# Latent projections in a new order, grouped keys copied out first, and both key parts in one 512-column score product, in a four-layer decoder on one core

## The chip, the cores and the metric

One core of one Trainium2 chip runs the whole program. The metric is the time of one execution in microseconds (us) on the device. The kernel before took 2579.66 us, the median of three runs (2578.66 to 2579.76).

## What is computed

The reference is a decoder trunk of four layers on a sequence of 256 positions with 2048 features, all in float32. The layers mix the positions in three ways, in the order latent, sparse, window, latent. Each layer has one input projection, its own heads, four heads of attention over a memory of 256 rows, a gate, and one output projection:

```python
def reference(x, mem, ...):
    mem_n = _rmsnorm(mem, mem_norm)
    for i in range(DEPTH):
        h = _rmsnorm(x, norm_in[i])
        kind, j = i % N_MIXERS, i // N_MIXERS
        if kind == 0:
            self_out, mq, gate = _mla_branch(h, w_in_a[j], a_q_norm[j], w_uq[j], a_kv_norm[j], w_ukv[j])
        elif kind == 1:
            self_out, mq, gate = _dsa_branch(h, w_in_b[j], rel_bias)
        else:
            self_out, mq, gate = _swa_branch(h, w_in_c[j], c_sinks[j], rel_bias)
        mem_out = _memory_attention(mq, mem_n @ w_mem_kv[i])
        y = jnp.concatenate([self_out, mem_out], axis=-1) * jax.nn.silu(gate)
        x = x + y @ w_out[i]
    return _rmsnorm(x, final_norm)
```

In a latent layer 16 heads get their queries from a compressed query stream (1536 features, weights w_uq) and their keys and values from a compressed stream (512 features, weights w_ukv):

```python
    q = (_rmsnorm(c_q, q_norm) @ w_uq).reshape(B, S, A_HEADS, A_NOPE + A_ROPE)
    kv = (_rmsnorm(c_kv, kv_norm) @ w_ukv).reshape(B, S, A_HEADS, A_NOPE + A_V)
    ...
        s = (jnp.einsum('bqhd,bkhd->bhqk', qn, k_nope, preferred_element_type=jnp.float32)
             + jnp.einsum('bqhd,bkd->bhqk', qr, k_rope, preferred_element_type=jnp.float32)) * scale
```

The sparse and the window layer have 32 query heads in four groups that share keys and values, and add a relative-position bias to the scores. The sparse layer also has a small indexer, whose products choose 64 keys for each query. Softmax, the product with the values, the gate and the output projection are alike in all.

## The kernel before

**Numbers in pairs.** TensorE multiplies numbers of reduced precision (fp32r), so a float32 number is kept as two, a high and a low part: `split` (L67) makes the high part by a copy on ACT (L60) and the low part by a subtraction on DVE (L69). A product of two matrices is then three: high by high, high by low, low by high.

**The stream of weights.** All weights flow through the core once. `stage` (L210) loads a block over SyncE's queue into one of five buffers; the queue follows the order of the program. `parts_of` splits 512 columns of it into wh and wl, with three buffers each. TensorE reads them at once: `rows_by` (L244) makes six products of 512 columns of such a part (L261, L262, L263), `columns_by` (L266) makes four of 512 (L282, wh by both parts of the input) and four of 256 (L286, wl by the high part). The result goes to an accumulator in PSUM with the tag "acc", of which there are **two**. Whoever asks for a third waits until the first is read out. Small results, scores among them, go to four other buffers, tag "mp".

**Reading an accumulator.** `head_parts` (L319) makes a pair from an accumulator of `columns_by`, which keeps high and low sums apart: a copy on ACT, a subtraction on DVE (L323, tile zl) and an addition on DVE (L324).

**A latent part.** Each of the two latent layers runs four parts of four heads. `Latent.project` makes the queries in two halves (12 blocks of features, tile qn), the keys in two halves (4 blocks, kn), the values (`rows_by`, va and vf), in every second part the rotary queries (acc_qr), and the gate (acc_g). `Latent.attend` then makes scores, softmax and outputs.

**A grouped layer.** `Grouped.first` makes keys and values (acc_kv). `dup` writes the keys twice beside each other, as high and low parts (hl), from the accumulator, for transposing (tile tr, then kd); the values are copied to vs, from the same accumulator, behind the keys of their block. The indexer of the sparse layer follows (acc_iq, L306, L309).

**Scores and softmax.** The 256 positions are two blocks b of 128. For b = 0 only 128 keys count: one product takes the high and the low part of 128 keys, 256 columns side by side, and DVE adds the halves (L542). For b = 1 the high and the low part of 256 keys are 256 columns each, and TensorE sums them itself, as separate products into the same 256 columns (L762 latent, L956 grouped, L602 memory). DVE then makes the sum with bias or mask and its extreme in one pass (L544, or L603 in the memory heads), ACT the exponential (L549, L554, L607).

**What sets the order.** The program runs the parts 4, 0, 1, 2, 3, 5 (4 and 5 are the memory heads) and puts the output projection of the part before (`w_out`, acc_wo, added to xc by DVE at L1149) behind the attention of the next. Inside, a scheduler orders each engine's instructions by their expected times; the loads on SyncE's queue stay as written.

Of the kernel before, what the change touches and what calls it, by code (L numbers as in the profile page):

```python
# [8 lines left out]
F32 = mybir.dt.float32  # L9
# [22 lines left out]
def kernel(ctx: ExitStack, tc: tile.TileContext, a: dict, out: bass.AP,  # L32
# [20 lines left out]
    def f32(ap):  # L53
        return ap.bitcast(F32)
# [272 lines left out]
    class Norm:  # L327
# [37 lines left out]
        def finish(self):  # L365
# [5 lines left out]
            nc.vector.tensor_scalar(self.eighth, self.rstd, 0.125, None, op0=OP.mult)  # L371
            half = small("xh", 2)
# [157 lines left out]
    def masked_softmax(score, bias, scale=None, nsk=None):  # L530
# [5 lines left out]
        for b in range(2):  # L536
# [4 lines left out]
            if b == 0:  # L541
                nc.vector.tensor_add(u[:, :n], sp[:, n:2 * n], bi)  # L542
                bi = u[:, :n]
            nc.vector.tensor_tensor_reduce(u[:, :n], sp[:, :n], bi, -1.0,  # L544
# [46 lines left out]
    def memory_attend(nm, kT, v, qT, gT):  # L591
        y = act.tile([P, 2, 4, S], F32R, name="y", tag="y", bufs=2)
        for h in range(2):
            es = []
            mn, sm = small("mn", 2), small("sm", 2)
            for b in range(2):
                sp = misc("msp")
                qs = slice(b * P, (b + 1) * P)
                seq = [(qT[h][:, u, k, qs], kT[h][:, v_, k, :])
                       for k in range(2) for u, v_ in ((0, 0), (0, 1), (1, 0))]  # L600
                for n_, (l, r_) in enumerate(seq):
                    nc.tensor.matmul(sp[:, :S], l, r_, start=n_ == 0, stop=n_ == len(seq) - 1)  # L602
                nc.vector.tensor_reduce(mn[:, b:b + 1], sp[:, :S], AX.X, OP.max, negate=True)  # L603
# [3 lines left out]
                nc.scalar.activation(e, sp[:, :S], AF.Exp, bias=ms[:, :1], scale=nm.col("rstd", b),  # L607
# [34 lines left out]
    class Latent:  # L642
# [79 lines left out]
        def project(self, g):  # L722
# [7 lines left out]
            for half in range(2):  # L730
                acc = columns_by(self.cT[:3], 12, wq, 0, (g * 768 + half * 384, 2, 192, 0, A_NOPE), "qn")
                q = act.tile([P, 2, 2, S], F32R, name="qn", tag="pq", bufs=PQ)
                head_parts(q, acc)
                qn.append(q)
            for half in range(2):
                acc = columns_by(self.cT[3:], 4, wkv, 0, (g * 1024 + half * 512, 2, 256, 0, A_NOPE), "kn")
                k = act.tile([P, 2, 2, S], F32R, name="kn", tag="pq", bufs=PQ)
                head_parts(k, acc)
                kn.append(k)
            acc = rows_by(self.cT[3:], 4, wkv, 0, (g * 1024, 4, 256, A_NOPE, A_NOPE), "va")  # L740
            split(v[:, 0, :], v[:, 1, :], acc[:, 0, :])
            copy_act(vf, acc[:, 1, :])
            if g % 2 == 0:
                self.rotary(g)
            return qn, self.qr[g % 2], kn, (v[:, 0], v[:, 1], vf), gate(self.nm, self.w, self.g0 + g * 512)

        def attend(self, qn, qr, kn, v, gT):
            y = act.tile([P, 2, 4, S], F32R, name="y", tag="y", bufs=2)
            for h in range(4):
                def score(b):  # L750
# [6 lines left out]
                    else:  # L757
                        seq = [(q[:, 0, z, qs], k[:, 0, z, :]), (q[:, 0, z, qs], k[:, 1, z, :]),
                               (q[:, 1, z, qs], k[:, 0, z, :]),
                               (qr[:, h, qs], self.kr[:, 0, :]), (qr[:, h, qs], self.kr[:, 1, :])]  # L760
# [475 lines left out]
```

## Time and profile before

| | |
|---|---|
| median of three runs | 2579.66 us |
| the profiled execution | 2579.56 us |
| its span in the trace | 2577.8 us |
| TensorE (PE) | busy 2560.7 us, 14176 products |
| VectorE (DVE) | busy 1900.4 us, 3780 instructions |
| ScalarE (ACT) | busy 1596.3 us, 3240 instructions |
| GpSimd (POOL) | busy 81.9 us |

The span lies 1.8 us below the profiled execution's own time; that stretch is in no trace. PE is TensorE's products, PEld its loads of the stationary operand, which run beside the products. SP is SyncE. L282 is line 282 of the kernel; a name such as acc_kn<-cT,wh is the tile written and the tiles read.

### The profile page before, as it was taken

Reading aid. Unit: us, or ns where it says so; the run is one execution under the profiler, and the core shown is the slowest. Engines: PE = TensorE matmul, PEld = TensorE weight load, DVE = VectorE, ACT = ScalarE, POOL = GpSimd, SP = SyncE. Lnnn points to the kernel's source line nnn. Section 1 sums busy time; section 2 is a strip of 40 time slices with the busy share of each in tenths; the row PEclk is TensorE's granted clock in tenths of the full one; section 3 lists DMA queues with packets and bytes.
Section 4 is the critical chain, followed back from the end, with each engine's and each line's share of the span. In section 5 each row is a group of like instructions: output and inputs, shape, how many; then the busy total and the mean of one; then the engine's idle time right before and its main releaser. Section 6 shows DMA issues by size and latency. Waiting matters only on the chain.

```text
span 2577.8 us, 41377 instructions
## 1 busy us (share of the span) xinstructions
PE 2560.7 (99%) x14176; PEld 2213.9 (86%) x14176; DVE 1900.4 (74%) x3780; ACT 1596.3 (62%) x3240; POOL 81.9 (3%) x151
## 2 busy tenths in 40 slices
PE   9999999999999999999999999999999999999998
PEld 7888888888888889888888888888888888888887
DVE  6666667677777687988887777878867767777666
ACT  6556556556565566666676566666756656666555
POOL 1000000000000000000000000000000000000000
PEclk9999999999999999999999999999999999999999
DMA  9888778666667777566666575565655768676755
GB/s 300 250 264 259 245 213 236 172 180 189 196 187 220 204 219 228 170 197 184 208 188 188 172 220 172 173 188 165 199 161 163 233 186 208 195 193 172 218 168 186
DMA packets 477747, 519.99 MB, mean 202 GB/s; under 512 B 69424, under 2 KB 389824, under 8 KB 475872
## 3 DMA queue, kind: packets, MB, share of 16 engines
q1 hardware_dynamic: 460080, 449.71, 59.5%
q0 software_dynamic: 16736, 66.65, 8.0%
q8 instruction: 111, 1.82, 0.3%
q10 hardware_dynamic: 720, 0.98, 0.1%
q14 instruction: 100, 0.82, 0.1%
HBM read 494.10 MB, written 35.75 MB: 206 GB/s over the span
## 4 chain that ended last, share of the span: by engine, by line
PE 96%; DVE 2%; ACT 1%; DMA 0%; issue 0%; SPq 0%; ACTq 0%; DVEq 0%
PE acc_g L282 14%; PE acc_g L286 7%; PE acc_wo L262 7%; PE acc_wo L261 7%; PE acc_wo L263 7%; PE acc_mq L282 5%; PE acc_q L282 5%; PE acc_mk L282 5%; PE acc_cq L282 3%; PE acc_qn L282 3%; PE acc_mq L286 2%; PE acc_q L286 2%; PE acc_mk L286 2%; PE acc_mv L262 2%; PE acc_mv L261 2%; PE acc_mv L263 2%
## 5 line engine op out<-in xcount | busy, mean ns | idle before, releaser
L60 ACT ACTIVATE wh<-wr 128x512 fp32r<-128x512 f32 (+1 forms) x1712 | 1064.5, 623 | 864.7 <-PE acc_g L282 167.5
L69 DVE TENSOR_TENSOR wl<-wr,wh 128x512 fp32r<-128x512 f32 (+1 forms) x1712 | 1157.6, 679 | 590.1 <-ACT wh L60 564.0
L282 PE MATMUL acc_g<-xT,wh 128*128 128x512 f32 x1536 | 484.5, 397 | 0.0
L286 PEld LDWEIGHTS acc_g<-xT,wl 128*128 128x128 f32 x1536 | 278.5, 188 | 59.3 <-DVE wl L69 2.4
L286 PE MATMUL acc_g<-xT,wl 128*128 128x256 f32 x1536 | 307.7, 282 | 0.2
L262 PE MATMUL acc_wo<-wl,y 128*128 128x512 f32 x752 | 297.6, 396 | 0.0
L263 PE MATMUL acc_wo<-wh,y 128*128 128x512 f32 x752 | 293.5, 390 | 0.0
L261 PE MATMUL acc_wo<-wh,y 128*128 128x512 f32 x752 | 293.4, 393 | 0.0
L282 PEld LDWEIGHTS acc_g<-xT,wh 128*128 128x128 f32 x1536 | 235.1, 189 | 0.6
L261 PEld LDWEIGHTS acc_wo<-wh,y 128*128 128x128 f32 x752 | 140.9, 188 | 28.0
L263 PEld LDWEIGHTS acc_wo<-wh,y 128*128 128x128 f32 x752 | 141.4, 188 | 27.0
L262 PEld LDWEIGHTS acc_wo<-wl,y 128*128 128x128 f32 x752 | 141.3, 188 | 26.2 <-DVE wl L69 0.4
L282 PE MATMUL acc_q<-xT,wh 128*128 128x512 f32 x512 | 161.9, 397 | 0.0
L282 PE MATMUL acc_mq<-xT,wh 128*128 128x512 f32 x512 | 161.2, 396 | 0.0
L282 PE MATMUL acc_mk<-mT,wh 128*128 128x512 f32 x512 | 161.1, 396 | 0.2 <-DVE mv L425 0.2
L282 PE MATMUL acc_cq<-xT,wh 128*128 128x512 f32 x384 | 120.8, 396 | 0.0
L282 PE MATMUL acc_qn<-cT,wh 128*128 128x512 f32 x384 | 120.5, 395 | 0.0
L1149 DVE TENSOR_TENSOR xc<-xc,acc_wo 128x1024 f32<-128x1024 f32 x92 | 112.0, 1217 | 7.2 <-PE acc_wo L263 6.4
L286 PEld LDWEIGHTS acc_mk<-mT,wl 128*128 128x128 f32 x512 | 96.0, 188 | 22.9 <-DVE wl L69 0.4
L286 PEld LDWEIGHTS acc_q<-xT,wl 128*128 128x128 f32 x512 | 94.0, 188 | 20.5
L286 PEld LDWEIGHTS acc_mq<-xT,wl 128*128 128x128 f32 x512 | 94.0, 188 | 20.4
L286 PE MATMUL acc_q<-xT,wl 128*128 128x256 f32 x512 | 101.9, 280 | 0.0
(324 smaller groups left out, 4264.8 us busy)
## 6 DMA issues: line engine op xcount, KB each, us to landing
wr<-in_w_out_dram SPq DMA_DIRECT2D x188, 512.0 KB, 3.7
wr<-in_w_in_a_dram SPq DMA_DIRECT2D x176, 512.0 KB, 4.5
wr<-in_w_mem_kv_dram SPq DMA_DIRECT2D x120, 512.0 KB, 4.6
wr<-in_w_in_b_dram SPq DMA_DIRECT2D x116, 512.0 KB, 3.8
wr<-in_w_in_c_dram SPq DMA_DIRECT2D x104, 512.0 KB, 3.6
wr<-in_w_uq_dram SPq DMA_DIRECT2D x192, 128.0 KB, 2.7
wr<-in_w_uq_dram SPq DMA_DIRECT2D x48, 256.0 KB, 3.9
tab<-flat POOLq DMA_DIRECT2D x8, 1536.0 KB, 9.3
```

Source lines behind the costliest of these rows:

```text
L60: inst = nc.scalar.activation(o, i, AF.Copy, scale=scale)
L69: nc.vector.tensor_sub(lo, src, f32(hi))
L261: nc.tensor.matmul(acc[t][:, :n], xh, wh[:, :n], start=first, stop=False)
L262: nc.tensor.matmul(acc[t][:, :n], xh, wl[:, :n], start=False, stop=False)
L263: nc.tensor.matmul(acc[t][:, :n], xl, wh[:, :n], start=False, stop=last)
L282: nc.tensor.matmul(acc[j], wh[:, o:o + P], q[:, :, kt % 4, :], start=kt == 0, stop=False)
L286: nc.tensor.matmul(acc[j][:, 0, :], wl[:, o:o + P], q[:, 0, kt % 4, :], start=False, stop=kt == kts - 1)
L1149: nc.vector.tensor_add(xs, xs, acc)
```

## The change

Five edits. `masked_softmax` adds the second half of the scores for both blocks, and the latent and grouped scores of block 1 take both parts of the keys in one product of 512 columns. `memory_attend` does so too: ACT copies the second half out, DVE sums and finds the extreme in one pass, and the exponential reads that sum, with the sign turned by a new vector `neg` of the norm. `Latent.project` runs keys 0, queries 0, values, keys 1, queries 1. `Grouped.first` copies keys (ks) and values (vs) of both blocks out of the accumulator before anything else, with the norm's factor, and `dup` splits ks. The loads of w_uq and w_ukv on SyncE's queue move with the projections.

```diff
@@ -369,6 +369,8 @@
             rsqrt_mean(self.rstd, s2, D)
             self.eighth = small("x8", 2, bufs=3)
             nc.vector.tensor_scalar(self.eighth, self.rstd, 0.125, None, op0=OP.mult)
+            self.neg = small("xn", 2, bufs=3)
+            nc.vector.tensor_scalar(self.neg, self.rstd, -1.0, None, op0=OP.mult)
             half = small("xh", 2)
             nc.vector.tensor_scalar(half, self.rstd, 0.5, None, op0=OP.mult)
             self.half = wk.tile([P, S], F32, name="half", tag="half", bufs=1)
@@ -538,10 +540,8 @@
             sp = score(b)
             u = wk.tile([P, S], F32, name="u", tag="e", bufs=4)
             bi = bias(b, n)
-            if b == 0:
-                nc.vector.tensor_add(u[:, :n], sp[:, n:2 * n], bi)
-                bi = u[:, :n]
-            nc.vector.tensor_tensor_reduce(u[:, :n], sp[:, :n], bi, -1.0,
+            nc.vector.tensor_add(u[:, :n], sp[:, n:2 * n], bi)
+            nc.vector.tensor_tensor_reduce(u[:, :n], sp[:, :n], u[:, :n], -1.0,
                                            nsk if nsk is not None else BIG,
                                            op0=OP.add, op1=OP.min, accum_out=mn[:, b:b + 1])
             e = wk.tile([P, S], F32, name="e", tag="e", bufs=4) if nsk is None else u
@@ -596,15 +596,17 @@
             for b in range(2):
                 sp = misc("msp")
                 qs = slice(b * P, (b + 1) * P)
-                seq = [(qT[h][:, u, k, qs], kT[h][:, v_, k, :])
-                       for k in range(2) for u, v_ in ((0, 0), (0, 1), (1, 0))]
-                for n_, (l, r_) in enumerate(seq):
-                    nc.tensor.matmul(sp[:, :S], l, r_, start=n_ == 0, stop=n_ == len(seq) - 1)
-                nc.vector.tensor_reduce(mn[:, b:b + 1], sp[:, :S], AX.X, OP.max, negate=True)
+                for k in range(2):
+                    nc.tensor.matmul(sp, qT[h][:, 0, k, qs], kT[h][:, :, k, :], start=k == 0, stop=False)
+                    nc.tensor.matmul(sp[:, :S], qT[h][:, 1, k, qs], kT[h][:, 0, k, :], start=False, stop=k == 1)
+                u = wk.tile([P, S], F32, name="u", tag="e", bufs=4)
+                copy_act(u, sp[:, S:])
+                nc.vector.tensor_tensor_reduce(u, sp[:, :S], u, -1.0, BIG,
+                                               op0=OP.add, op1=OP.min, accum_out=mn[:, b:b + 1])
                 ms = small("ms", 2)
                 nc.vector.tensor_mul(ms[:, :1], mn[:, b:b + 1], nm.col("rstd", b))
                 e = wk.tile([P, S], F32, name="e", tag="e", bufs=4)
-                nc.scalar.activation(e, sp[:, :S], AF.Exp, bias=ms[:, :1], scale=nm.col("rstd", b),
+                nc.scalar.activation(e, u, AF.Exp, bias=ms[:, :1], scale=nm.col("neg", b),
                                      accum_out=sm[:, b:b + 1])
                 es.append(e)
             r = small("rc", 2)
@@ -727,19 +729,24 @@
 
             v = act.tile([P, 2, 512], F32R, name="va", tag="aux", bufs=AUX)
             vf = spare(g % 2, "vf")
-            for half in range(2):
+
+            def keys(half):
+                acc = columns_by(self.cT[3:], 4, wkv, 0, (g * 1024 + half * 512, 2, 256, 0, A_NOPE), "kn")
+                kn.append(act.tile([P, 2, 2, S], F32R, name="kn", tag="pq", bufs=PQ))
+                head_parts(kn[half], acc)
+
+            def queries(half):
                 acc = columns_by(self.cT[:3], 12, wq, 0, (g * 768 + half * 384, 2, 192, 0, A_NOPE), "qn")
-                q = act.tile([P, 2, 2, S], F32R, name="qn", tag="pq", bufs=PQ)
-                head_parts(q, acc)
-                qn.append(q)
-            for half in range(2):
-                acc = columns_by(self.cT[3:], 4, wkv, 0, (g * 1024 + half * 512, 2, 256, 0, A_NOPE), "kn")
-                k = act.tile([P, 2, 2, S], F32R, name="kn", tag="pq", bufs=PQ)
-                head_parts(k, acc)
-                kn.append(k)
+                qn.append(act.tile([P, 2, 2, S], F32R, name="qn", tag="pq", bufs=PQ))
+                head_parts(qn[half], acc)
+
+            keys(0)
+            queries(0)
             acc = rows_by(self.cT[3:], 4, wkv, 0, (g * 1024, 4, 256, A_NOPE, A_NOPE), "va")
             split(v[:, 0, :], v[:, 1, :], acc[:, 0, :])
             copy_act(vf, acc[:, 1, :])
+            keys(1)
+            queries(1)
             if g % 2 == 0:
                 self.rotary(g)
             return qn, self.qr[g % 2], kn, (v[:, 0], v[:, 1], vf), gate(self.nm, self.w, self.g0 + g * 512)
@@ -755,11 +762,11 @@
                         seq = [(q[:, 0, z, qs], k[:, :, z, :P]), (q[:, 1, z, qs], k[:, :, z, :P]),
                                (qr[:, h, qs], self.kr[:, :, :P])]
                     else:
-                        seq = [(q[:, 0, z, qs], k[:, 0, z, :]), (q[:, 0, z, qs], k[:, 1, z, :]),
-                               (q[:, 1, z, qs], k[:, 0, z, :]),
-                               (qr[:, h, qs], self.kr[:, 0, :]), (qr[:, h, qs], self.kr[:, 1, :])]
+                        seq = [(q[:, 0, z, qs], k[:, :, z, :]), (q[:, 1, z, qs], k[:, 0, z, :]),
+                               (qr[:, h, qs], self.kr)]
                     for n_, (l, r_) in enumerate(seq):
-                        nc.tensor.matmul(sp[:, :S], l, r_, start=n_ == 0, stop=n_ == len(seq) - 1)
+                        n = r_.shape[-1] * (r_.shape[1] if len(r_.shape) == 3 else 1)
+                        nc.tensor.matmul(sp[:, :n], l, r_, start=n_ == 0, stop=n_ == 2)
                     return sp
                 tp = masked_softmax(score, lambda b, n: caus[:, S - n:], self.scale)
                 pT = wk.tile([P, 768], F32R, name="pT", tag="pT", bufs=PT)
@@ -789,11 +796,14 @@
             self.k = act.tile([P, 4, 2, S], F32R, name="kd", tag="big0")
             vs = act.tile([P, 4, S], F32, name="vs", tag="aux", bufs=AUX)
             self.v, self.sel = vs[:, :2, :], vs[:, 2:, :]
+            ks = tmp("ks").rearrange("p (t c) -> p t c", t=2)
             for t in range(2):
                 sc = nm.col("rstd", t)
+                copy_act(ks[:, t, :], acc[:, t, :S], scale=sc)
+                copy_act(self.v[:, t, :], acc[:, t, S:], scale=sc)
+            for t in range(2):
                 self.dup(lambda i0, i1: self.k.rearrange("p g v s -> p (g v) s")
-                         [:, i0:i1, t * P:(t + 1) * P], acc[:, t, :S], sc, 4)
-                copy_act(self.v[:, t, :], acc[:, t, S:], scale=sc)
+                         [:, i0:i1, t * P:(t + 1) * P], ks[:, t, :], 4)
             if self.sparse:
                 steps.append(self.select())
             else:
@@ -809,16 +819,14 @@
                 hi, lo = (self.vz[z][:, t, 64:].rearrange("p (g c) -> p g c", c=P)[:, :, :64] for z in range(2))
                 split(hi, lo, self.v[:, t, :].rearrange("p (g c) -> p g c", c=64))
 
-        def dup(self, dst, src, sc, n):
+        def dup(self, dst, src, n):
 
             s3 = src.rearrange("p (g d) -> p g d", g=n)
             for g0 in range(0, n, 2):
                 m = min(2, n - g0)
                 hl = part_tile()[:].rearrange("p (g v e d) -> p g v e d", g=2, v=2, e=2)
                 for d in range(2):
-                    copy_act(hl[:, :m, 0, d, :], s3[:, g0:g0 + m], scale=sc)
-                    nc.vector.scalar_tensor_tensor(hl[:, :m, 1, d, :], s3[:, g0:g0 + m], sc,
-                                                   f32(hl)[:, :m, 0, d, :], op0=OP.mult, op1=OP.subtract)
+                    split(hl[:, :m, 0, d, :], hl[:, :m, 1, d, :], s3[:, g0:g0 + m])
                 transposed(lambda i0, i1: dst(2 * g0 + i0, 2 * g0 + i1),
                            [hl[:, g, v].rearrange("p a b -> p (a b)")
                             for g in range(m) for v in range(2)])
@@ -949,12 +957,8 @@
                 def score(b):
                     sp = misc("sp")
                     qb = q[h // 4][:, h % 4, b * P:(b + 1) * P]
-                    if b == 0:
-                        nc.tensor.matmul(sp[:, :S], qb, self.k[:, g, :, :P], start=True, stop=True)
-                    else:
-                        for v in range(2):
-                            nc.tensor.matmul(sp[:, :S], qb, self.k[:, g, v, :],
-                                             start=v == 0, stop=v == 1)
+                    n = (b + 1) * P
+                    nc.tensor.matmul(sp[:, :2 * n], qb, self.k[:, g, :, :n], start=True, stop=True)
                     return sp
 
                 def bias(b, n):
```

DVE, in the projections of a latent part (L323 and L324 clear the accumulators of queries and keys, qn and kn; va are the values). Before:

```order
L69 TENSOR_TENSOR wl<-wr,wh 128x512 x5
L323 TENSOR_TENSOR zl<-acc_qn,qn 128x512
L69 TENSOR_TENSOR wl<-wr,wh 128x512
L324 TENSOR_TENSOR qn<-zl,acc_qn 128x512
L69 TENSOR_TENSOR wl<-wr,wh 128x512
L323 TENSOR_TENSOR zl<-acc_kn,kn 128x512
L324 TENSOR_TENSOR kn<-zl,acc_kn 128x512
L69 TENSOR_TENSOR wl<-wr,wh 128x512 x2
L323 TENSOR_TENSOR zl<-acc_kn,kn 128x512
L324 TENSOR_TENSOR kn<-zl,acc_kn 128x512
```

The same place with the change:

```order
L69 TENSOR_TENSOR wl<-wr,wh 128x512 x5
L323 TENSOR_TENSOR zl<-acc_qn,qn 128x512
L69 TENSOR_TENSOR wl<-wr,wh 128x512
L324 TENSOR_TENSOR qn<-zl,acc_qn 128x512
L69 TENSOR_TENSOR wl<-wr,wh 128x512 x2
L69 TENSOR_TENSOR va<-acc_va,va 128x512
L69 TENSOR_TENSOR wl<-wr,wh 128x512 x3
L323 TENSOR_TENSOR zl<-acc_kn,kn 128x512
L69 TENSOR_TENSOR wl<-wr,wh 128x512
L324 TENSOR_TENSOR kn<-zl,acc_kn 128x512
L69 TENSOR_TENSOR wl<-wr,wh 128x512 x5
```

Before, the queries' passes are followed by those of the keys at a distance of one weight part; with the change the values' pass stands between queries and keys.

ACT, at the start of the sparse layer (hl are the doubled keys, kd their transposed form, vs the values, ks the new copy of the keys). Before:

```order
L60 ACTIVATE wh<-wr 128x512 x12
L60 ACTIVATE hl<-acc_kv,xr 128x2x64
L60 ACTIVATE wh<-wr 128x512
L60 ACTIVATE hl<-acc_kv,xr 128x2x64
L60 ACTIVATE wh<-wr 128x512 x2
L60 ACTIVATE hl<-acc_kv,xr 128x2x64
L60 ACTIVATE wh<-wr 128x512
L60 ACTIVATE hl<-acc_kv,xr 128x2x64
L60 ACTIVATE kd<-tr 128x4x128
L60 ACTIVATE wh<-wr 128x512
L60 ACTIVATE vs<-acc_kv,xr 128x256
```

The same place with the change:

```order
L60 ACTIVATE wh<-wr 128x512 x12
L60 ACTIVATE ks<-acc_kv,xr 128x256
L60 ACTIVATE vs<-acc_kv,xr 128x256
L60 ACTIVATE ks<-acc_kv,xr 128x256
L60 ACTIVATE vs<-acc_kv,xr 128x256
L60 ACTIVATE wh<-wr 128x512
L60 ACTIVATE hl<-ks 128x2x64 x4
L60 ACTIVATE wh<-wr 128x512 x3
L60 ACTIVATE kd<-tr 128x4x128
L60 ACTIVATE hl<-ks 128x2x64 x2
```

The reads of acc_kv, before spread between weight copies, now stand together at the head, and the splits of ks stand four in a row behind one weight copy.

DVE, in a head of the sparse layer, around the pass over an output chunk (xc; bs is the bias with the selection, u the sum, mn its extreme). Before:

```order
L69 TENSOR_TENSOR wl<-wr,wh 128x512
L544 ISA u,mn<-sp,bs 128x256
L544 ISA mn 128x1
L69 TENSOR_TENSOR pT_12641<-ptp,pT_12640 128x3x128
L1149 TENSOR_TENSOR xc<-xc,acc_wo 128x1024
L965 TENSOR_TENSOR bs<-bm,vs 128x128
L69 TENSOR_TENSOR wl<-wr,wh 128x512
```

Such a place with the change:

```order
L69 TENSOR_TENSOR wl<-wr,wh 128x512
L544 ISA u,mn<-sp,u 128x128
L544 ISA mn 128x1
L969 TENSOR_TENSOR bs<-bm,vs 128x256
L543 TENSOR_TENSOR u<-sp,bs 128x256
L544 ISA u,mn<-sp,u 128x256
L544 ISA mn 128x1
L1153 TENSOR_TENSOR xc<-xc,acc_wo 128x1024
L969 TENSOR_TENSOR bs<-bm,vs 128x128
L69 TENSOR_TENSOR wl<-wr,wh 128x512
```

The new pass L543 on 128x256 stands between two weight splits, together with the passes of both blocks and the output chunk.

## Rows read from the trace of the kernel before

**Rows 1.** The page: busy time of each engine, and the chain that ended last.
```profile
PE 2560.7 (99%) x14176; PEld 2213.9 (86%) x14176; DVE 1900.4 (74%) x3780; ACT 1596.3 (62%) x3240; POOL 81.9 (3%) x151
...
PE 96%; DVE 2%; ACT 1%; DMA 0%; issue 0%; SPq 0%; ACTq 0%; DVEq 0%
```
**Rows 2.** Waits of TensorE: line, waited for, total us, times, longest us.
```profile
PE acc_kn L282 <- ACT wh L60: 4.1, 8, 0.5
...
PE acc_iq L306 <- ACT vs L60: 1.0, 1, 1.0
```
**Rows 3.** Timeline at one latent part's keys: start, us, engine, line, operation, tiles.
```profile
526.69 0.63 ACT L60 ACTIVATE wh<-wr 128x512 fp32r<-128x512 f32 x1 [0.76 <-DVE wl L69]
526.72 0.62 PE L282 MATMUL acc_kn<-cT,wh 128*128 128x512 f32 x2
...
527.23 0.58 ACT L60 ACTIVATE qn<-acc_qn 128x512 fp32r<-128x512 f32 x1
...
529.28 0.39 PE L286 MATMUL acc_kn<-cT,wl 128*128 128x256 f32 x2
529.36 0.68 DVE L324 TENSOR_TENSOR qn<-zl,acc_qn 128x512 fp32r<-128x512 f32 x1
...
530.19 0.70 PE L282 MATMUL acc_kn<-cT,wh 128*128 128x512 f32 x2 [0.52 <-ACT wh L60]
```
**Rows 4.** The chain of waits at two places: start, us, what, count.
```profile
476.53 0.71 PE msp L602 x6
...
519.22 0.47 PE acc_qn L282 x2
```
**Rows 5.** Timeline at the values of the same part.
```profile
533.06 0.40 PE L261 MATMUL acc_va<-wh,cT 128*128 128x512 f32 x1
...
538.51 0.39 PE L261 MATMUL acc_qr<-wh,cT 128*128 128x512 f32 x1
...
540.61 0.58 ACT L60 ACTIVATE vf<-acc_va 128x512 f32<-128x512 f32 x1
```
**Rows 6.** Timeline in a head of the sparse layer.
```profile
1218.45 1.22 DVE L1149 TENSOR_TENSOR xc<-xc,acc_wo 128x1024 f32<-128x1024 f32 x1 [0.65 <-PE acc_wo L263]
...
1219.59 1.29 DVE L69 TENSOR_TENSOR wl<-wr,wh 128x512 fp32r<-128x512 f32 x2
...
1220.47 0.40 PE L262 MATMUL acc_wo<-wl,y 128*128 128x512 f32 x1
```
**Rows 7.** Groups of instructions by shape: busy us, mean ns | idle before, releaser.
```profile
L965 DVE TENSOR_TENSOR bs<-bm,vs 128x256 f32<-128x256 f32 x32 | 13.4, 418 | 0.0
L603 DVE TENSOR_REDUCE mn<-msp 128x1 f32<-128x256 f32 x32 | 13.1, 418 | 0.4 <-PE msp L602 0.4
L544 DVE DVE_READ_ACCUMULATOR2_ANT mn<- 128x1 f32 x192 | 15.9, 83 | 0.0
L60 ACT ACTIVATE pT<-ptp 128x256 fp32r<-128x256 f32 x32 | 12.3, 384 | 5.9 <-PE ptp L517 5.7
L607 ACT ACTIVATE e<-msp,ms,xr 128x256 f32<-128x256 f32 x32 | 17.7, 554 | 3.3 <-DVE ms L605 3.3
L554 ACT ACTIVATE e<-u,ms,qsn 128x256 f32<-128x256 f32 x32 | 18.9, 590 | 5.2 <-DVE ms L553 5.2
```
**Rows 8.** Busy time in the sparse and the window layer's heads: PE, PEld, DVE, ACT, POOL.
```profile
1098.00:1420.00 322.00, 322.00 (x1799) 277.89 (x1798) 263.68 (x589) 219.64 (x477) 9.37 (x13) 1.00 0.65 193
1590.00:1900.00 310.00, 310.00 (x1726) 267.05 (x1725) 248.01 (x568) 210.80 (x496) 3.80 (x5) 1.00 0.58 179
```
**Rows 9.** Timeline at the start of the sparse layer.
```profile
986.68 0.39 PE L263 MATMUL acc_kv<-wh,xT 128*128 128x512 f32 x1
...
998.37 0.48 ACT L60 ACTIVATE vs<-acc_kv,xr 128x256 f32<-128x256 f32 x1
998.73 0.61 ACT L60 ACTIVATE kd<-tr 128x512 fp32r<-128x512 f32 x1
998.90 0.62 PE L306 MATMUL acc_iq<-xT,wh 128*128 128x384 f32 x2 [1.04 <-ACT vs L60]
```

## The prediction

> **What bounds the kernel now.** I read the page first. TensorE is busy for 2560.7 us of a span of 2577.8 us, and the chain of work that ended last is 96% TensorE [rows 1]. So the time is TensorE's own products plus its holes, and a part of the change counts only where it shortens a product, closes a hole or opens one. What is not product time is 17.1 us in all, so closing holes can't give more than that.
>
> Next the waits. Of the holes with a name behind the start-up, I look at two: the keys of the latent layers (4.1 us in 8 places) and the indexer's products (1.0 us, once) [rows 2]. The change touches both places. The sum below is made against the profiled execution, 2579.56 us; the median of the runs shown is 2579.66 us, so the one can stand for the other.
>
> **The keys' wait is not what its row says.** The row names the copy of a weight (wh). But the wh that the waiting product reads was written from 526.69 us on and took 0.63 us; it was long there at 530.19 us, when the product came [rows 3]. What ended just then is VectorE's last pass over the second queries, at 529.36 + 0.68 = 530.04 us [rows 3]. There are two accumulators, so the second keys need the one that the second queries held. Between the two lies only the first half of the keys, 8 products of 512 and 8 of 256 columns: 8 x 0.235 + 8 x 0.118 = 2.8 us [rows 4]. Clearing the queries (a copy on ACT, a subtraction and an addition on DVE, with splits of weights between them, as the order shown with the change has them) ended 530.04 - 526.72 = 3.3 us behind the first product of the keys [rows 3].
>
> The loss at one place: the last pair of 256 columns starts at 529.28 us, so the next product was due 2 x 0.118 us later, at 529.51. It came at 530.19, and its pair took 0.70 us where the pair of 526.72 took 0.62 [rows 3]. That is 0.68 + 0.07 = 0.75 us. Eight places (the second keys of four parts in each of two latent layers) make **6.0 us**. The idle time of the wait row alone, 4.1 us, is the lower bound.
>
> **Part 1, the new order of the projections.** Keys 0, queries 0, values, keys 1, queries 1. The products that wait for the clearing of queries 0 are now keys 1, and between lie the values: from 533.06 to 538.51 us in the trace, 5.45 us [rows 5], against the 3.3 us of the clearing. That wait should go: **-6.0 us**.
>
> What is late next? Queries 1 take the accumulator of the values, whose last copy (vf) ended at 540.61 + 0.58 = 541.19 us, 2.68 us behind the values' end [rows 5], and keys 1 cover it for 2.8 us. That is the thinnest margin of the change, 0.1 us. If the copy came 0.3 us later, eight places would give back 8 x 0.2 = 1.6 us; I keep this for the range and not in the sum. Queries 0 need the accumulator of the output projection ahead of them, which one DVE addition clears (1.22 us for such a chunk [rows 6]); keys 0 cover it for 2.8 us, enough for one split of a weight ahead of it as well: nothing. The loads of these weights move along on SyncE's queue, in the order of the products, with the same bytes; no row of TensorE names a load as the releaser. Cost nothing; if loads came late, a row would name a DMA.
>
> **Part 2, fewer and wider products.** The columns stay the same. 192 pairs of 256 columns become one product of 512 each: two in each of 32 latent heads, one in each of 64 grouped heads, two in each of 32 memory blocks. Six score products of 256 took 0.71 us, 118 ns each; two of 512 took 0.47 us, 235 each [rows 4], and the values' 24 products in 5.45 us make 227 [rows 5]. So 236 ns give way to 227 to 235 ns. I take 5 ns, the middle: **-1.0 us** (range -0.2 to -1.7). The weight loads that go with them cost nothing now, since products follow each other at 118 ns. The Trainium skill, "TensorEngine Tiling (Array Packing)", section "Instruction Overhead", says that each matmul carries about 60 cycles of overhead; by that rule this part would be larger, and these rows speak against it.
>
> **Part 3, what VectorE and ScalarE get for it.** The second half of the scores must now be added: 96 additions of 128x256 at 0.418 us by the nearest row, the bias addition of the same shape [rows 7]. That is 40.1 us of DVE: 13.4 in each grouped layer, 6.7 in the heads of each latent one. In the memory blocks a reduction of 0.418 us becomes a pass with two inputs, which I take to be as long, and a read of 0.083 us; ACT gets a copy, 0.384 us by the nearest row, and its exponential reads from another memory, 0.590 in place of 0.554 [rows 7]: 0.42 x 32 = 13.4 us of ACT, over eight memory parts. Is there room? In the heads of the sparse layer DVE is busy 263.7 and ACT 219.6 of 322 us, in the window layer 248.0 and 210.8 of 310 [rows 8]. With 13.4 us more, DVE stands at 86% and 84%.
>
> What counts is the tightest place. In the sparse layer DVE passes over an output chunk and then makes two low halves, the first of which is done at 1219.59 + 0.64 = 1220.23 us; the product that reads it starts at 1220.47 [rows 6]. So 0.2 us of slack, at two such places in each of 4 parts. An addition of 0.42 us that falls there costs 0.2 us: 8 x 0.2 = 1.6 us. Bounds of the whole part: 0, if every addition lies in idle time, and 26.8 us, if all 64 grouped additions are seen. I take **+0.8 us**, half of the tight places, near the lower bound, since TensorE has no hole in either grouped window [rows 8]: bursts of passes are taken up now. I allow 3 in the forecast's own range.
>
> **Part 4, grouped keys and values copied out first.** In the sparse layer the second chunk of the indexer waits 1.04 us for the accumulator of keys and values, whose last copy (vs) ends at 998.85 us, some 11.8 us behind the last product that starts at 986.68 [rows 9]; with the slow restart I count 1.2. Now four copies, of which one follows the other by some 0.36 us (998.37 to 998.73 [rows 9]), stand at the head of ACT's line, and the accumulator is free some 1.5 us behind its last product: -1.2. But these copies and the first four splits now stand in one line, ahead of the next weights. Four more copies of 0.36 are 1.4 us in which no weight is copied, and the three buffers of weights take part of it. I expect a new hole of 0.8 us there (0 to 1.5), and one of 0.3 us at the same place of the window layer (0 to 0.6): **-0.1 us** together. The vector of negated factors, of two elements and four times in all, costs nothing, since it is made with its likes at the norms.
>
> **The sum.** -6.0 - 1.0 + 0.8 - 0.1 = -6.3 us; 2579.6 - 6.3 = **2573.3 us**, 0.24% faster. A measurement of this kernel can tell about 0.2% from no change, 5.2 us, so faster means below 2574.4.
>
> **Rivals.**
> 1. *The additions show.* DVE runs late oftener than at the eight tight places and gives back 2 to 6 us in place of 0.8: 2574.5 to 2578.5. For it: DVE at 86% in the sparse layer, and in the changed order the passes of a whole block and an output chunk stand between two splits. Against: no hole in either grouped window now. Chance 0.19.
> 2. *The new order of projections wins nothing.* If the row were right, and ACT itself late at the second keys, or if queries 1 waited as long behind the values as the keys did, the 6.0 us stay: 2579.3. For it: the row's name, and a margin of 0.1 us. Against: the time at which that weight was written. Chance 0.10.
> 3. *Slower: VectorE becomes the bound of the grouped heads.* Place: the 64 heads. Price: each addition in full, 26.8 in place of 0.8 us: 2599.3. It decides from the point at which DVE's work of a head, with its share of the splits, is longer than TensorE's. Against: DVE has 58 us of 322 idle in the sparse layer and would use 13.4 of them. Chance 0.04.
> 4. *Each product has a fixed part that falls away whole.* The granted clock is 1.00 in both grouped windows [rows 8], which is 2.4 GHz; 256 columns are 107 ns of the 118, so 11 ns at most by these rows: 192 x 11 = 2.1 in place of 1.0 us, 2572.2. Against: 512 columns are 213 of their 227 to 235 ns, so the wide product has as large a part or a larger one. Chance 0.05. By the skill's rule above, 60 cycles at 2.4 GHz are 25 ns, an estimate, and the sum would be 2569.5.
>
> **How the numbers follow.** The forecast has 0.62; its own range is 2571.5 to 2575.5 (no new holes on one side, the thin margin or 3 us of additions on the other). The range 2569.5 to 2578.5 holds the forecast, rival 4 and rival 1, with a us or two below for holes that close beside the two I priced. Faster by over 0.2%: some five sixths of 0.62, and rival 4, 0.56. Slower by over 0.2%: 0.04. Within 0.2%: the rest, 0.40.
>
> **What would show it.** Right: no row of TensorE at the keys waiting for wh, and none at the queries or the values in its place; TensorE's count 192 lower, its busy time about 1 us lower; DVE's busy time some 40 us higher; no wait of the indexer for vs, but a small one there for wh or wl. Wrong: a row at the queries with eight waits of 0.2 us or more (the margin), a row at the low halves of the output projection or the gate with tens of places (the additions), or a row at the keys as before.

## The result and the profile after

The changed kernel took **2595.46 us**, the median of six runs (2594.49 to 2596.93), against 2579.61 us of the kernel before in the same comparison: ratio 1.0063, interval 1.0053 to 1.0073. It is 16 us slower. I had forecast 2573.3 us and a range up to 2578.5, and had given "slower" a chance of 0.04.

Where the time went, by layer: the start of the last product of each layer's output projection in either trace, and how far the distance between the two traces grew within the layer.

| layer | end before, us | growth in the changed kernel, us |
|---|---|---|
| 0, latent | 963.8 | -4.4 |
| 1, sparse | 1491.5 | +14.4 |
| 2, window | 1970.6 | +8.5 |
| 3, latent | 2569.4 | -3.1 |

The latent layers won 7.6 us. The grouped layers lost 22.9.

The page of the changed kernel, busy times and chain; they answer to [rows 1]:

```profile
PE 2566.4 (99%) x13984; PEld 2208.4 (85%) x13984; DVE 1928.8 (74%) x3912; ACT 1611.5 (62%) x3276; POOL 82.9 (3%) x151
...
PE 94%; DVE 3%; ACT 2%; DMA 1%; issue 0%; SPq 0%; POOL 0%; ACTq 0%; DVEq 0%
```

TensorE has 192 products fewer and is busy *longer*, by 5.7 us. The chain now passes through DVE and ACT for 5% of the span, against 3%. DVE's busy time rose by 28 us; the added passes last 0.42 us each, 40 us in sum as forecast, but the busy time counts overlapping records once.

Its waits, against [rows 2]:

```profile
PE ptp L519 <- ACT e L60: 5.6, 2, 3.3
PE acc_g L282 <- DVE mqT L324: 5.1, 2, 2.6
PE o L986 <- ACT pT L60: 2.2, 3, 1.0
PE ptp L519 <- ACT u L60: 1.3, 1, 1.3
...
PE acc_iq L306 <- ACT wh L60: 0.4, 1, 0.4
```

The keys' row of eight waits is gone, and the indexer's wait for vs gave way to a smaller one for wh, as forecast. New are a few long waits at transposes of a head (ptp), at outputs (o) and at the first gate product (acc_g).

All of these new waits lie at two places, the ends of the sparse and of the window layer's heads. Windows of the changed kernel there (columns as in [rows 8]: length, then busy PE, PEld, DVE, ACT, POOL, then the granted clock):

```profile
1400.00:1410.00 10.00, 8.98 (x54) 7.58 (x53) 7.43 (x20) 6.53 (x15) 0.00 (x0) 1.00 0.53 161
1410.00:1420.00 10.00, 3.80 (x16) 2.44 (x14) 4.73 (x18) 4.65 (x14) 0.90 (x1) 0.77 0.32 106
1420.00:1430.00 10.00, 7.43 (x25) 5.98 (x25) 4.46 (x8) 1.82 (x3) 2.05 (x2) 0.55 0.06 15
1430.00:1440.00 10.00, 10.00 (x60) 8.75 (x59) 5.87 (x14) 6.89 (x16) 0.00 (x0) 1.00 0.51 153
...
1895.00:1930.00 35.00, 30.54 (x156) 25.65 (x155) 20.07 (x45) 18.76 (x44) 0.00 (x0) 0.85 0.38 119
```

TensorE is idle for 40 - 30.2 = 9.8 us at the first place and 35 - 30.5 = 4.5 at the second, 14.3 in all. The rest of the 22.9 us is some 8 to 9 us: the granted clock fell to 0.77 and 0.55 of full speed in the stretches with the holes and just behind them, and products run there at the lower of the two levels. In the kernel before the clock is 1.00 in both grouped windows [rows 8] and in the first place's stretch:

```profile
1400.00:1440.00 40.00, 40.00 (x246) 35.50 (x245) 26.27 (x51) 22.89 (x45) 3.52 (x4) 1.00 0.66 198
```

The timeline of the first place has six output products that take 1.22 us at 1395.98, and six such products that take 2.45 at 1419.55:

```profile
1395.98 1.22 PE L986 MATMUL o<-pT,vz 128*128 128x512 f32 x6
...
1407.26 0.40 PE L286 MATMUL acc_mq<-xT,wl 128*128 128x256 f32 x2
1407.49 0.49 PE L519 MATMUL ptp<-ident,e 128*128 128x128 f32 x3
1409.00 0.50 PE L986 MATMUL o<-pT,vz 128*128 128x512 f32 x1 [1.02 <-ACT pT L60]
...
1413.00 0.33 PE L519 MATMUL ptp<-ident,e 128*128 128x128 f32 x1 [2.32 <-ACT e L60]
...
1417.22 0.48 PE L519 MATMUL ptp<-ident,e 128*128 128x128 f32 x1 [3.30 <-ACT e L60]
...
1419.55 2.45 PE L986 MATMUL o<-pT,vz 128*128 128x512 f32 x6 [0.58 <-ACT pT L60]
1422.04 0.69 DVE L992 TENSOR_TENSOR yt<-o,gT 128x512 f32<-128x512 f32 x1 [1.95 <-PE o L986]
1422.65 1.28 DVE L323 TENSOR_TENSOR zl<-acc_mq,mqT 128x512 f32<-128x512 f32 x2
...
1423.85 0.68 DVE L324 TENSOR_TENSOR mqT<-zl,acc_mq 128x512 fp32r<-128x512 f32 x1
1424.58 1.22 PE L282 MATMUL acc_g<-xT,wh 128*128 128x512 f32 x2 [2.57 <-DVE mqT L324]
```

The last weight products of the memory queries (acc_mq) end at 1407.5 us. From there the last two heads run bare: transposes wait for ACT's normalized exponentials, outputs for the weights' copies. No products of weights fill in, since the next ones, the gate's, need an accumulator, and both hold memory queries, which DVE clears behind the last head (zl, mqT at 1422.65). In the kernel before these heads stood among the weight products: the sparse layer's last scores started at 1400.1 us, the memory queries' products ran until 1416.8, and TensorE had no hole there.

So the heads came too late. The view of one line's instructions, for the score products, gives the first and the last start in each grouped layer; before, then changed:

```profile
L953 PE MATMUL sp<-kd,qS x32: 278/364/365, 1106.6 to 1400.1; 128*128 128x256 f32 x32
...
L953 PE MATMUL sp<-kd,qS x32: 278/364/365, 1585.6 to 1878.4; 128*128 128x256 f32 x32
```

```profile
L961 PE MATMUL sp<-kd,qS x64: 276/376/404, 1101.7 to 1413.3; 128*128 128x256 f32 x32, 128*128 128x512 f32 x32
...
L961 PE MATMUL sp<-kd,qS x64: 276/376/402, 1596.0 to 1899.7; 128*128 128x256 f32 x32, 128*128 128x512 f32 x32
```

In the sparse layer the first head starts 4.9 us earlier, mostly by what layer 0 won, and the last 13.2 us later. From first to last it is 293.5 us before and 311.6 now (block 1 of the last head included, 0.2 us), 0.6 us per head on average. DVE's added pass is 0.42 us. And yet TensorE had no long hole on the way: the heads fell behind the stream of weight products, which ran ahead in their place, until there were none left.

Where were they late: on the chip, or in the order? TensorE's products stand in an order that the scheduler fixed when the program was built, from expected times. Its wait rows above name a transpose at three places in the whole run. At an earlier head of the changed kernel:

```profile
1215.94 0.79 ACT L60 ACTIVATE e<-e,rc 128x128 f32<-128x128 f32 x2
...
1218.16 0.27 PE L519 MATMUL ptp<-ident,e 128*128 128x128 f32 x1
1218.19 0.60 PE L961 MATMUL sp<-kd,qS 128*128 128x256 f32 x2
```

The normalized exponentials are ready at 1215.94 + 0.79 = 1216.73 us, and the first transpose that reads them comes 1.4 us later, behind weight products. In the first 30 heads of the sparse layer this distance is 1.3 to 3.3 us, 2.2 in the median; in the kernel before it is 2.2 as well. It is longer than the added pass, so these heads were not late on the chip: the new order puts them later among the weight products. The last two ran bare, and each had its exponentials normalized 4.0 to 4.5 us after its scores, the pass included.

### The profile page after: what moved, and what is told of

It reads as the page before. It is cut to its first block, busy times and chain, and to the rows that moved or that the text cites. A ratio compares the mean times of both kernels' runs of the same rounds, so it can differ in the third digit from the quotient of the medians.

```text
span 2593.1 us, 41168 instructions
## 1 busy us (share of the span) xinstructions
PE 2566.4 (99%) x13984; PEld 2208.4 (85%) x13984; DVE 1928.8 (74%) x3912; ACT 1611.5 (62%) x3276; POOL 82.9 (3%) x151
## 4 chain that ended last, share of the span: by engine, by line
PE 94%; DVE 3%; ACT 2%; DMA 1%; issue 0%; SPq 0%; POOL 0%; ACTq 0%; DVEq 0%
PE acc_g L282 14%; PE acc_g L286 7%; PE acc_wo L261 7%; PE acc_wo L262 7%; PE acc_wo L263 7%; PE acc_q L282 5%; PE acc_mk L282 5%; PE acc_mq L282 4%; PE acc_qn L282 3%; PE acc_cq L282 3%; PE acc_q L286 2%; PE acc_mk L286 2%; PE acc_mv L262 2%; PE acc_mv L263 2%; PE acc_mv L261 2%; PE acc_mq L286 2%
## 5 line engine op out<-in xcount | busy, mean ns | idle before, releaser
L286 PEld LDWEIGHTS acc_mk<-mT,wl 128*128 128x128 f32 x512 | 96.0, 188 | 22.9 <-DVE wl L69 0.4
```

Of the source, the lines that this page charges most:

```text
L286: nc.tensor.matmul(acc[j][:, 0, :], wl[:, o:o + P], q[:, 0, kt % 4, :], start=False, stop=kt == kts - 1)
```

## The experiments

My theory at this point: a grouped head is a **chain** (scores, sum, extreme, exponential, normalizing, transposes), and in TensorE's order the next head's scores mostly stand right behind the first transposes of the head before (median distance 0.03 us in both traces). So heads follow one another at the length of the chain, and the added pass lengthens it past what the weight products of a head cover. (By the distances above, the covered heads had time to spare on the chip; their chain can have acted only as the scheduler expected it, through the order.) The main rival was **volume**: DVE, at 86%, has too much to do. Another: one of the other edits displaces the heads.

**Which edit.** The first two runs split the change at the grouped scores. The first adds them to the kernel before:

```diff
-                    if b == 0:
-                        nc.tensor.matmul(sp[:, :S], qb, self.k[:, g, :, :P], start=True, stop=True)
-                    else:
-                        for v in range(2):
-                            nc.tensor.matmul(sp[:, :S], qb, self.k[:, g, v, :],
-                                             start=v == 0, stop=v == 1)
+                    n = (b + 1) * P
+                    nc.tensor.matmul(sp[:, :2 * n], qb, self.k[:, g, :, :n], start=True, stop=True)
```

> The kernel before with one edit: the grouped heads of block 1 take both key parts in one product and DVE adds the halves. Theory (chain): a grouped head is a chain from its scores to its transposes, the next head's scores stand right behind those, and the added pass makes the chain longer than the weights' stream that covers it; the heads fall behind and the last ones run uncovered. Then this edit alone brings the holes of the changed kernel at the ends of the sparse and the window layer: 2598 to 2605 us, slower than the change as a whole, which has its gains of about 8 us in the latent layers beside it. Rival (volume): VectorE has too much to do; the same. Rival (the order of projections, the copies or the memory heads displace the heads): 2577 to 2582 us.

Measured: 2603.56 us, ratio 1.0094 (1.0079 to 1.0109). By layer: +0.0, +14.5, +8.0, 0.0 us, the loss of the whole change and nothing else. The second run undoes that edit in the changed kernel (the diff above from + to -, and `masked_softmax` adds in block 1 for the latent heads alone).

> The changed kernel with the grouped scores as before, two products and no added pass; all other edits stay. Theory (chain) and rival (volume): the holes at the ends of the two grouped layers go and the gains stay, about 8 us in the latent layers: 2569 to 2573 us. Rival (other edits displace the heads): the holes stay, 2590 to 2596 us.

Measured: 2572.90 us, ratio 0.9977 (0.9967 to 0.9988). By layer: -4.1, -0.2, +0.5, -3.2. All of the loss is the grouped scores' edit; the rest of the change is a gain of 6.3 us (2579.20 in the same comparison).

**Chain or volume.** The next two leave the products of the kernel before alone and add one DVE pass of the same shape per head, in the chain or beside it:

```diff
+            if b == 1 and scale is None:
+                nc.vector.tensor_tensor(u, u, u, op=OP.max)
             e = wk.tile([P, S], F32, name="e", tag="e", bufs=4) if nsk is None else u
```

```diff
+            if b == 1 and scale is None:
+                xd = wk.tile([P, S], F32, name="xd", tag="xd", bufs=1)
+                nc.vector.tensor_tensor(xd, bi, bi, op=OP.max)
             e = wk.tile([P, S], F32, name="e", tag="e", bufs=4) if nsk is None else u
```

> The kernel before, products unchanged, with one more DVE pass of 128x256 in each grouped head of block 1, in the chain: the sum is compared with itself (the larger of u and u, so no value changes) before the exponential reads it. Theory (chain): heads fall behind in the sparse layer as in the changed kernel, holes at its end: 2590 to 2600 us. Rival (volume): the same. Rival (the wide product itself, or its longer hold of a score buffer, is the cause): 2579 to 2582 us.

> The kernel before with the same DVE pass of 128x256 in each grouped head of block 1, but beside the chain: it reads the bias and writes a tile that nobody reads. Theory (chain): the heads keep step in the sparse layer, 2579 to 2584 us. Rival (volume): as slow as with the pass in the chain, 2590 to 2600 us.

Measured: 2591.47 us in the chain, ratio 1.0048 (1.0033 to 1.0063); 2580.78 us beside it, ratio 1.0007 (0.9998 to 1.0017), not to be told from no change. The pages' busy times, in the chain and beside it:

```profile
PE 2564.7 (99%) x14176; PEld 2216.3 (86%) x14176; DVE 1918.4 (74%) x3844; ACT 1597.7 (62%) x3240; POOL 81.7 (3%) x151
```

```profile
PE 2561.1 (99%) x14176; PEld 2214.5 (86%) x14176; DVE 1919.8 (74%) x3844; ACT 1596.8 (62%) x3240; POOL 81.7 (3%) x151
```

DVE has as many instructions and as much busy time in both. In the sparse layer volume falls. First and last scores of the sparse layer, in the chain and beside it:

```profile
L955 PE MATMUL sp<-kd,qS x32: 277/364/365, 1105.8 to 1411.9; 128*128 128x256 f32 x32
```

```profile
L956 PE MATMUL sp<-kd,qS x32: 277/364/365, 1106.4 to 1398.7; 128*128 128x256 f32 x32
```

306.1 us against 292.3. By layer the pass in the chain cost 10.0 us in the sparse but only 2.0 in the window layer, and the one beside it 1.9 there. So the window layer, where the change loses 8.5, doesn't tell the two theories apart in these runs; it was left open.

**The place in the chain.** This run has the pass where the change has it, ahead of the extreme, but no wide product:

```diff
+            src = sp[:, :n]
+            if b == 1 and scale is None:
+                nc.vector.tensor_add(u, sp[:, :n], bi)
+                src, bi = u, zero
-            nc.vector.tensor_tensor_reduce(u[:, :n], sp[:, :n], bi, -1.0,
+            nc.vector.tensor_tensor_reduce(u[:, :n], src, bi, -1.0,
```

> The kernel before, products unchanged, with the additional pass where the changed kernel has it: in each grouped head of block 1, DVE first adds bias and scores (128x256, read from the score buffer), and the pass that finds the extreme reads that sum and a tile of zeros. Open is why the pass behind the extreme cost 2.0 us in the window layer and the change 8.5. Theory (chain): it is the place in the chain, so this loses 10 us or more in the sparse and 7 to 9 in the window layer, 2596 to 2604 us. Rival (the wide product): the window layer loses 2 us as before, 2590 to 2593 us.

Measured: 2598.11 us, ratio 1.0074 (1.0051 to 1.0097). By layer: -0.4, +9.9, +7.8, 0.0. The window layer's loss comes back without any wide product: the place of the pass makes it. Its first and last scores there, with the pass behind the extreme and ahead of it:

```profile
L955 PE MATMUL sp<-kd,qS x32: 278/364/365, 1594.7 to 1891.4; 128*128 128x256 f32 x32
```

```profile
L959 PE MATMUL sp<-kd,qS x32: 278/364/365, 1595.1 to 1898.9; 128*128 128x256 f32 x32
```

Why a pass behind the extreme is cheaper there was not tried. Two things don't fit a chain that is simply too long. In the sparse layer the pass alone loses 9.9 us, and with the wide product 14.5 (the run with the grouped edit alone): some 4.6 us come with the rest of that edit, the wide product, and no run shows how. And counted from the layer's first head, the sparse heads of this run are 12 us later than in the kernel before by the thirteenth head and no later than that at the last, though each has the pass: from there on they keep step.

**Breaking the chain.** In the next run a head's scores and softmax stand ahead of the transposes of the head before, with six tiles of the softmax in place of four:

```diff
+            ahead = front(heads[0])
+            for n, h in enumerate(heads):
+                es = ahead
+                if n < 7:
+                    ahead = front(heads[n + 1])
+                tp = weights_T(es, [(0, 0), (1, 0), (1, 1)])
```

> The changed kernel, all edits in, but a grouped head's scores and softmax stand in the program ahead of the transposes of the head before (and six in place of four buffers for the tiles of the softmax), so that two heads overlap. Theory (chain): with the chain broken the added pass costs nothing; no hole at the ends of the grouped layers, the sparse layer's last scores well ahead of where they were: 2568 to 2573 us. Rival (volume, now of VectorE as a whole): still late, above 2580 us.

Measured: 2573.74 us, ratio 0.9979 (0.9969 to 0.9988), just outside the range expected and on the chain's side: by layer -3.7, +0.6, 0.0, -3.2, and the sparse layer's last scores start at 1376.8 us in place of 1413.3. All 64 added passes are in this kernel. With heads overlapping they cost nothing that shows.

> Scores ahead as in the run e5_scores_ahead, but the grouped scores of block 1 as before, two products and no added pass. Theory (chain): with the chain broken, wide product and added pass are worth what their products are, 64 times some 5 ns, so this is within 1.5 us of e5_scores_ahead: 2568 to 2573 us. If the pass still cost something, this is faster by 2 us or more.

Measured: 2575.09 us, ratio 0.9986 (0.9976 to 0.9996), above the range expected. It isn't faster than with the passes, and within 1.5 us of them; its own loss is in the sparse layer (+2.1 us) and was not looked into.

**Has the chain a reserve?** Wide product and pass in four of eight heads (`h % 2 == 0`), then in the first part of each grouped layer alone (`g == 0`):

> The changed kernel with the wide product and the added pass in four of eight grouped heads of each part (the even ones), the other four as before. Theory (chain, with a reserve): the heads have some reserve against the weights' stream, and half the passes stay within it, so hardly anything is lost: 2571 to 2576 us, no holes at the ends of the grouped layers. Rival (each pass costs its share): half of the some 23 us are lost, 2582 to 2586 us.

> The changed kernel with the wide product and the added pass in the heads of the first part of each grouped layer alone. Theory (chain, with a reserve): the heads fall behind in that part and catch up in the next three, whose products cover them; nothing lost at the end: 2571 to 2575 us. Rival (each pass costs its share, wherever it stands): a quarter of the some 23 us, 2577 to 2580 us.

Measured: 2571.98 us, ratio 0.9973 (0.9961 to 0.9984), and 2573.60 us, ratio 0.9978 (0.9967 to 0.9990). By layer: -3.4, -0.1, -0.7, -3.1, and -3.6, +2.2, +0.3, -3.2; the 2.2 us lie ahead of the heads, whose first score starts at 1105.4 us (1102.6 without any grouped edit). Both are on the side of a reserve: 32 of 64 passes cost nothing, where half of 22.9 us would be 11. The second gives the reserve a size: in its sparse layer the heads are 7.5 us late after the first part and level again fourteen heads later, so without the pass they catch up some 0.5 us per head (an estimate). A pass of 0.42 us in every head uses nearly all of that. The stretch of the first hole, with half of the heads:

```profile
1400.00:1440.00 40.00, 40.00 (x238) 35.07 (x237) 26.71 (x54) 24.63 (x52) 3.51 (x4) 1.00 0.63 197
```

No hole, full clock. This is the lowest median here, though not to be told from that without any grouped edit (2572.90).

**What the runs leave open.** Each of these edits changed the chain and, with it, the order that the scheduler made of it. No run kept the order of the kernel before and added the pass. That the order carries the loss rests on the traces: the transposes' operands lay ready in all but the last heads.

**The order of projections alone**, on the kernel before:

> The kernel before with the new order of the latent projections alone. If the eight waits at the keys were those for the clearing of the queries, at 0.75 us each: 2573 to 2574 us, no wait row at the keys, none at the queries or values. If the row was right that ACT's copy of a weight ended them: 2578 to 2580 us.

Measured: 2576.38 us, ratio 0.9989 (0.9980 to 0.9998), a miss between the two figures. By layer: -1.6, -0.3, 0.0, -0.9. The eight waits at the keys are gone, but four others have come: the queries wait for vf, the values' last copy.

```profile
PE acc_qn L282 <- ACT vf L60: 2.0, 4, 0.5
```

The timeline at one of the four shows why: two exponentials of a latent head stand on ACT between the values' two copies.

```profile
624.64 0.60 ACT L60 ACTIVATE va<-acc_va 128x512 fp32r<-128x512 f32 x1 [1.35 <-PE acc_va L263]
...
625.66 0.48 ACT L554 ACTIVATE e<-u,ms,qsn 128x128 f32<-128x128 f32 x1
...
626.14 0.59 ACT L554 ACTIVATE e<-u,ms,qsn 128x256 f32<-128x256 f32 x1
...
627.25 0.58 ACT L60 ACTIVATE vf<-acc_va 128x512 f32<-128x512 f32 x1
627.87 0.73 PE L282 MATMUL acc_qn<-cT,wh 128*128 128x512 f32 x2 [0.49 <-ACT vf L60]
```

The copy ends 627.83 - 624.22 = 3.6 us behind the start of the last values product (624.22), and keys 1 cover only 3.2 of it (627.87 - 0.49 - 624.22). This is the thin margin of part 1, broken at four of eight places: by the part, layer 0 won 1.0, 0.0, 0.8 and 0.0 us. In the changed kernel the same copy ends 2.6 to 3.0 us behind, at all eight.

## Why the prediction was wrong

**Part 1, the order: right in mechanism, and in size in the changed kernel.** The row at the keys named the copy of a weight; the wait went when the order was changed and nothing was done to that copy. One reading was wrong, without harm: the copy of 526.69 us, which I took for the waiting product's, served the pairs before it. Theirs is the next one, and the one that ended just ahead of the wait's end served still later products, since its low half was made only from 530.14 on, until 530.83, and theirs is read at 530.72:

```profile
528.08 0.63 ACT L60 ACTIVATE wh<-wr 128x512 fp32r<-128x512 f32 x1 [0.28 <-PE acc_kn L282]
...
529.48 0.63 ACT L60 ACTIVATE wh<-wr 128x512 fp32r<-128x512 f32 x1 [0.76 <-PE acc_kn L282]
...
530.14 0.69 DVE L69 TENSOR_TENSOR wl<-wr,wh 128x512 fp32r<-128x512 f32 x1
```

So the product's weight was ready at 528.71 us, 1.5 us before it started. The latent layers won 7.6 us, where 6.0 were counted for the order and some 0.5 for their share of the products; what the rest is was not tried. The margin behind the values was named and decides: it held in the changed kernel and broke in half the places with the order alone.

**Part 2, the products: small, as forecast, perhaps less.** A latent head's eight score products took 0.95 us before and its six take 0.95 after, in the view of the chain that ended last. The Trainium skill's rule ("TensorEngine Tiling (Array Packing)", "Instruction Overhead", about 60 cycles for each matmul) asks for two products' overhead less here; the trace doesn't show it. One latent head's scores of both blocks, before and after:

```profile
597.67 0.95 PE sp L762 x8
```

```profile
597.23 0.95 PE sp L769 x6
```

**Part 3, the passes: the step that failed.** The term was +0.8 us; the grouped layers lost 22.9 us, all of it with the grouped scores' edit. I priced it with two questions: has DVE idle time, and how much slack has a weight's low half at the tightest place? Both were about the stream of weights, and on it the answers hold: the low halves cost nothing to speak of. The question left out was what a longer head does to TensorE's order, and what then still covers the last heads. "TensorE has no hole in either grouped window" was my argument that bursts are taken up. It could not show this, since a late head leaves no hole while weight products stand in its place; the debt falls due only at the end. There the last two heads of the sparse layer ran bare, and the window layer's end had the same waits: 14.3 us of idle time and a lower clock.

The pace of the heads doesn't show what they had in reserve. Before, they followed each other every 9.5 us (293.5 / 31), and the output projections of two parts of eight heads lie 76.6 us apart, 9.6 per head; but heads that keep step with the weights have their pace, whatever they need themselves. The catching up of some 0.5 us per head, against a pass of 0.42, is the better measure. It explains why heads with the pass hardly catch up, and not where the distance comes from: why the sparse heads lose 12 us in the first twelve is open.

Rival 3 had the place (the 64 heads) and the sign. Its mechanism was wrong: DVE's volume, at a price of 26.8 us, where it was the pass's place in the chain and so in the order. That the 22.9 us measured are near its price is luck: they are holes at two places and a lower clock, not 64 shares.

The order of the changed kernel's TensorE, known before, had it in plain view at the end of the sparse layer, where I hadn't looked:

```
L286 MATMUL acc_mq<-xT,wl 128x256 x2
L519 MATMUL ptp<-ident,e 128x128 x3
...
L961 MATMUL sp<-kd,qS 128x256
L961 MATMUL sp<-kd,qS 128x512
...
L519 MATMUL ptp<-ident,e 128x128
L961 MATMUL sp<-kd,qS 128x256
L961 MATMUL sp<-kd,qS 128x512
L519 MATMUL ptp<-ident,e 128x128 x3
...
L282 MATMUL acc_g<-xT,wh 128x512 x2
```

Two heads' scores stand between the last products of the memory queries and the gate's first, with no weight product among them.

**Part 4, the copies: about right.** The wait for vs (1.0 us) went and one for wh of 0.4 came. By layers the run without the grouped edit has -0.2 and +0.5 us in the two grouped layers; -0.1 in all was forecast. It has the other edits of these layers in it too, so the copies' own share isn't shown.

## What to carry to other kernels

Where one stream of work covers another in an order fixed beforehand, the cover's idle time and its tightest place are only half the account: ask also where a longer chain puts the covered work in that order, and what still covers its end. Here the pass cost nothing in half of the heads or in the first part's alone. In all of them the runs lost 12 to 23 us in the grouped layers, depending on its place in the chain and on the wide product, and the loss showed as a hole only where the cover ended. To tell a late order from a late chain, look how long an operand lay ready when the engine took it. Read the order of the instructions at the end of each stage, and let two turns overlap if the covered work ends last.

## What the hardware did that I had not expected

A hole cost more than its length. TensorE idled 14.3 us at the two places, and with the clock granted at 0.55 to 0.85 of full speed around them the layers lost 22.9. The kernels without the holes have 1.00 in the same stretch.
